# The retention's output product of a two-layer decoder as one block product of seven, behind the second gates

## The chip, the core and the metric

The kernel runs on one core of a Trainium2 chip. What is measured is the device time in microseconds (us) of one execution. A core has a matrix engine (TensorE, PE in the profile), a vector engine (VectorE, DVE), a scalar engine (ScalarE, ACT), a general engine (GpSimd, POOL) and a queue engine that starts transfers (SyncE, SP). Each engine works off its own instructions in a fixed order and waits on semaphores for the others.

## The reference

Two layers over 512 tokens with a width of 1024, all in fp32. Each layer mixes an attention branch and a retention branch through two gates, and a feed-forward part of width 4096 follows. The change touches the product of the retention's result `r` with `w_b`, and what stands around it:

```python
h = rmsnorm(x, g_mix)
z = h @ w_in
aq, ak, av, rq, rk, rv, rg, ga, gb = jnp.split(z, SPLIT_POINTS, axis=-1)
...
r = chunkwise_retention(rq, rk, rv)
r = r * lax.rsqrt(jnp.mean(r * r, axis=-1, keepdims=True) + EPS)
r = r.reshape(B, S, RET_V) * jax.nn.silu(rg.astype(jnp.float32))
yb = r.astype(x.dtype) @ w_b

mixed = jax.nn.sigmoid(ga) * ya + jax.nn.sigmoid(gb) * yb
x = x + mixed @ w_out
```

## The kernel before

Activations lie transposed: features on the 128 partitions, in 8 chunks of 128 features, and the 512 tokens along a row. A fp32 product is made of three matrix products of rounded parts: each operand is split into `hi` (rounded) and `lo` (the rest), and hi·hi, hi·lo and lo·hi are added up (`products`, lines 391 to 393).

**Weights.** They arrive in units of 128x1024 (512 KB), in the order of the list `order`. SP starts the load of a unit into a `raw` tile (five of them), four units ahead of the one that is split; ACT writes `hi` (line 339), DVE writes `lo` (line 340), each with four buffers, so that splitting stays up to three units ahead of PE. Units that are sums of others are made in two ways: DVE adds two raw tiles (line 319), or POOL sums blocks in DRAM in the course of the run, from a list of jobs (`sum_steps`), and SP loads the result.

**Products of seven.** Three products of the kernel already multiply 2x2 blocks with seven block products in place of eight: the values `rv` (function `values`), the feed-forward's first product (name `pair`) and its second (name `block`). They need forms of the moving operand, that is, sums and differences of its four blocks (two halves of the features by two halves of the tokens). For `values` the class `Turned` builds them: `load` fetches the input, `build` makes the sums on DVE (lines 892 to 895) and splits them, on ACT (line 411) and DVE (line 412).

**Retention.** Heads go in two pairs. Each of a pair's two heads ends in `norm` and `finish`: the squares `sq`, their split `sh` and `sl`, a column sum on PE (`ssq`, line 569), a square root on ACT (`inv`, line 570), a reciprocal on DVE (line 571), two products each (lines 1067 and 1068) and the split of the result (`r<-z` or `late<-z`, lines 411 and 412). This work runs as a generator in the background: every `chunk` of a foreground product advances it by some steps (its last argument is the rate), and `drain()` runs it to its end.

**The piece that is changed**, in each layer: the last two chunks of `rg`, with the second pair of heads as background; gates 0 to 3 (`chunk("w_in", ...)` with `gate`, which evacuates PSUM on DVE at line 827 and takes the sigmoid on ACT at line 828); `w_b` for output chunks 0 to 3 as a group over the eight input chunks, in the middle of which `second_pair` drains the retention; gates 4 to 7; `w_b` for chunks 4 to 7 one after the other; then `x` (which at this time holds the gated attention branch, `mixed`) is loaded again from DRAM, and `w_out` follows. Each `w_b` matmul has a 128x128 weight block and all 512 tokens moving, and there are 8 x 8 x 3 = 192 of them per layer. `put_mixed` multiplies the result by the gate (line 1176), adds the attention branch (1177) and splits the sum (411, 412).

The order of each engine's instructions is not written out: a scheduler of the framework sets it from its own estimates and from the order of the code, with `tc.issue_after` as a bound in a few places. On the chip each engine keeps to the order so found.

## Time and profile before

| what | us |
|---|---|
| median of 3 runs (1467.56 to 1468.66) | 1468.51 |
| the profiled execution | 1466.77 |
| its span, first to last instruction | 1465.0 |
| DVE busy | 1124.7 |
| ACT busy | 944.6 |
| POOL busy | 209.0 |

The span is what the profile sees of an execution; 1.8 us of the profiled one lie around it. A row of a group reads: line, engine, operation, output<-inputs, shapes, count, then the busy time, the mean duration of one in ns, and the engine's idle time before them with what ended it. A row of the timeline reads: start in us, duration in us, engine, line, operation, and in brackets the idle time of the engine before it and what ended that. Matmuls overlap, so their durations are longer than the distance from one start to the next.

### The profile page before, as it was taken

Reading aid. Unit: us, or ns where it says so; the run is one execution under the profiler, and the core shown is the slowest. Engines: PE = TensorE matmul, PEld = TensorE weight load, DVE = VectorE, ACT = ScalarE, POOL = GpSimd, SP = SyncE. Lnnn points to the kernel's source line nnn. Section 1 sums busy time; section 2 is a strip of 40 time slices with the busy share of each in tenths; the row PEclk is TensorE's granted clock in tenths of the full one; section 3 lists DMA queues with packets and bytes.
Section 4 is the critical chain, followed back from the end, with each engine's and each line's share of the span. In section 5 each row is a group of like instructions: output and inputs, shape, how many; then the busy total and the mean of one; then the engine's idle time right before and its main releaser. Section 6 shows DMA issues by size and latency. Waiting matters only on the chain.

```text
span 1465.0 us, 21388 instructions
## 1 busy us (share of the span) xinstructions
PE 1453.4 (99%) x7751; PEld 1256.2 (86%) x7751; DVE 1124.7 (77%) x1697; ACT 944.6 (64%) x1549; POOL 209.0 (14%) x302
## 2 busy tenths in 40 slices
...
GB/s 263 182 295 207 114 152 259 200 207 290 228 57 193 195 188 199 181 172 188 297 172 191 291 212 104 181 251 189 228 272 101 99 197 199 196 189 199 180 186 140
DMA packets 95867, 287.32 MB, mean 196 GB/s; under 512 B 11152, under 2 KB 11280, under 8 KB 90896
## 3 DMA queue, kind: packets, MB, share of 16 engines
...
q8 instruction: 61, 1.00, 0.3%
...
## 4 chain that ended last, share of the span: by engine, by line
PE 97%; DMA 1%; ACT 1%; DVE 0%; issue 0%; SPq 0%; DVEq 0%; ACTq 0%
PE mm L391 25%; PE mm L393 25%; PE mm L392 25%; PE b L391 3%; PE b L392 3%; PE b L393 3%; PE rv L391 2%; PE rv L392 2%; PE rv L393 2%; PE mm L406 1%; PE score L774 1%; PE pT L739 1%; PE r L393 1%; PE r L392 1%; PE r L391 1%; DMA y<-eu 1%
## 5 line engine op out<-in xcount | busy, mean ns | idle before, releaser
L339 ACT ACTIVATE hi<-raw 128x1024 fp32r<-128x1024 f32 (+1 forms) x375 | 382.3, 1020 | 285.3 <-PE mm L392 166.0
L340 DVE TENSOR_TENSOR lo<-raw,hi 128x1024 fp32r<-128x1024 f32 (+1 forms) x376 | 439.2, 1174 | 144.6 <-ACT hi L339 143.2
L391 PE MATMUL mm<-xh,hi 128*128 128x512 f32 (+1 forms) x976 | 344.1, 355 | 1.0 <-ACT xh L414 1.0
L392 PE MATMUL mm<-xl,hi 128*128 128x512 f32 (+1 forms) x976 | 344.0, 355 | 0.0
L393 PE MATMUL mm<-xh,lo 128*128 128x512 f32 (+1 forms) x976 | 341.9, 355 | 0.0
L393 PE MATMUL mm<-r,lo 128*128 128x256 f32 (+1 forms) x736 | 239.2, 325 | 0.5 <-DVE lo L340 0.5
L392 PE MATMUL mm<-r,hi 128*128 128x256 f32 (+1 forms) x736 | 239.3, 325 | 0.0
L391 PE MATMUL mm<-r,hi 128*128 128x256 f32 (+1 forms) x736 | 236.6, 325 | 0.5 <-ACT mm L1343 0.5
L391 PEld LDWEIGHTS mm<-xh,hi 128*128 128x128 f32 x976 | 184.8, 189 | 25.6 <-ACT xh L414 1.4
L392 PEld LDWEIGHTS mm<-xl,hi 128*128 128x128 f32 x976 | 184.9, 189 | 24.2
L393 PEld LDWEIGHTS mm<-xh,lo 128*128 128x128 f32 x976 | 183.9, 189 | 23.6
L391 PEld LDWEIGHTS mm<-r,hi 128*128 128x128 f32 x736 | 139.9, 190 | 13.7 <-ACT mm L1343 0.7
L392 PEld LDWEIGHTS mm<-r,hi 128*128 128x128 f32 x736 | 139.9, 190 | 13.2
L393 PEld LDWEIGHTS mm<-r,lo 128*128 128x128 f32 x736 | 139.9, 190 | 12.1 <-DVE lo L340 0.7
L1488 POOL DMA_DIRECT2D y<-eu x56 | 62.4, 1358 | 369.1 <-DVE eu L1473 369.1
L392 PE MATMUL mm<-lo,r 128*128 128x512 f32 (+1 forms) x276 | 104.4, 388 | 0.0
L393 PE MATMUL mm<-hi,r 128*128 128x512 f32 (+1 forms) x276 | 101.2, 387 | 0.0
L391 PE MATMUL mm<-hi,r 128*128 128x512 f32 (+1 forms) x276 | 98.7, 391 | 0.5 <-ACT r L411 0.2
L391 PE MATMUL b<-hi,r 128*128 128x512 f32 x180 | 70.5, 392 | 0.0
L392 PE MATMUL b<-lo,r 128*128 128x512 f32 x180 | 70.3, 391 | 0.0
L393 PE MATMUL b<-hi,r 128*128 128x512 f32 x180 | 67.9, 390 | 0.0
L1488 POOL DMA_DIRECT2D y<-y x56 | 55.6, 1007 | 78.7 <-ACT y L1483 73.5
...
## 6 DMA issues: line engine op xcount, KB each, us to landing
...
```

The lines of the kernel that those rows point to most:

```text
L339: state["high"] = nc.scalar.activation(hi[:, at], raw[:, at], AF.Copy).ins
L340: nc.vector.tensor_tensor(lo[:, at], raw[:, at], f32(hi[:, at]), ALU.subtract)
L391: nc.tensor.matmul(ps, ah, bh, start=start and i == 0, stop=False, **more)
L392: nc.tensor.matmul(ps, ah, bl, start=False, stop=False, **more)
L393: latest[0] = nc.tensor.matmul(ps, al, bh, start=False, stop=stop and i == n - 1, **more).ins
L406: latest[0] = nc.tensor.matmul(ps, w[:, cols(j, c)], moving[k][low], start=first, stop=bool(final)).ins
L739: nc.tensor.transpose(pt[:, i * P : (i + 1) * P], sm[:, at : at + P], ident)
L774: nc.tensor.matmul(ps[:, g * w : (g + 1) * w], q_s[g][:, c, at], part[:, keys], start=i == 0, stop=i == 1)
L1488: nc.gpsimd.dma_start(y[:, 2 * j + m, i * T : (i + 1) * T], t, **how)
```

## The change

The product with `w_b` becomes one product of seven block products, with 256 tokens moving in each matmul. The weight units of `w_b` come in the list `order` behind all of `w_in` under the name `wb`, 14 per layer: part 0 to 6, two units each. Parts 2 and 4 are made by DVE from raw tiles, parts 1 and 5 come from sums that POOL makes in DRAM (two more jobs per layer), parts 0, 3 and 6 are loaded as they are. Gates 0 to 3 and the last two chunks of `rg` advance the background by 1.5 steps per chunk, and the retention is drained behind gate 3; gates 4 to 7 follow in front of the product. Between them `again(0)` and `again(2)` build the forms of the retention's results: two DVE additions put hi and lo of the first pair's results together again, the second pair's results are there in fp32 in the tile that held `rg`, and `Turned.build` makes and splits the sums. `mixing` runs the seven products into three PSUM accumulators `a`, `b` and `c` of two banks each, and writes the mixed result in four quarters (`put`), from the forms and from plain quarters of `r` (`outputs`).

```diff
     order = [("w_in", i) for i in range(4 + 2 + 8 + 2 + 4 + 2 + 2)]
     order += [("w_a", i) for i in range(4)]
     order += [("rv", part, u) for part in range(7) for u in range(2)]
-    order += [("w_in", i) for i in range(24, 34)]
-    order += [("w_b", i) for i in range(4)]
-    order += [("w_in", i) for i in range(34, 38)]
-    order += [("w_b", i) for i in range(4, 8)]
+    order += [("w_in", i) for i in range(24, 38)]
+    order += [("wb", part, u) for part in range(7) for u in range(2)]
     order += [("w_out", i) for i in range(8)]
...
-    sums_rv = [dram.tile([2, P, 2 * UNIT], F32, name=f"sums_rv{l}") for l in range(DEPTH)]
+    MIXING = {"rv": w_rv, "wb": w_wb}
+    sums_mix = {
+        name: [dram.tile([2, P, 2 * UNIT], F32, name=f"sums_{name}{l}") for l in range(DEPTH)] for name in MIXING
+    }
...
+        for name, at in (("rv", 0), ("wb", 5)):
+            jobs[at:at] = [(sums_mix[name][layer][u], MIXING[name][layer, u], 2 * UNIT) for u in range(2)]
...
+        at = {0: 0, 1: 1, 3: 3, 5: 0, 6: 2}[part]
+        source = sums_mix[name][layer][u] if part in (1, 5) else MIXING[name][layer, u]
...
-            def build(self, ks):
-                for part, b in enumerate(self.b):
+            def build(self, ks, scaled=True):
+                two_b = self.b.pop(ks)
+                for part, b in enumerate(two_b if scaled else ()):
                     for i in range(2):
                         col = g_mix * KD + ks + 4 * part + i
                         nc.scalar.activation(b[:, i, :], b[:, i, :], AF.Copy, scale=gain[:, col : col + 1])
-                (b11, b12), (b21, b22) = ((b[:, :, :H], b[:, :, H:]) for b in self.b)
+                (b11, b12), (b21, b22) = ((b[:, :, :H], b[:, :, H:]) for b in two_b)
...
-                split(hi, lo, self.b[1].rearrange("p a (b t) -> p b a t", t=H))
...
-        rg, rg_next = {}, {}
         def put_rg(i):
             def put(ps):
                 if i % 2 == 0:
                     two = big("z")
                     rg[i], rg_next[i + 1] = two[:, 0, :], two[:, 1, :]
+                    rg_both[i] = two
...
         drain()
         background.append(retention(1))
         for i in (6, 7):
-            chunk("w_in", layer, xs, put_rg(i))
+            chunk("w_in", layer, xs, put_rg(i), 1.5)
         gates = []
 
-        def gate_tile(c):
-            if c % 2 == 0:
-                two = big("gb")
-                gates.extend(two[:, j, :] for j in range(2))
-
-        for c in range(4):
-            gate_tile(c)
-            chunk("w_in", layer, xs, gate(gates[c]))
-
-
+        def put_gates(cs, rate=1.0):
+            for c in cs:
+                if c % 2 == 0:
+                    gates.append(big("gb"))
+                chunk("w_in", layer, xs, gate(gates[c // 2][:, c % 2, :]), rate)
+
+        put_gates(range(4), 1.5)
+        drain()
+
+
+        turned = Turned()
+        turned.take()
+
+        def again(ks):
+            first = big("xg")
+            for i in range(2):
+                hi, lo = (f32(view(s)) for s in ret[ks + i])
+                nc.vector.tensor_tensor(first[:, i, :], hi, lo, ALU.add)
+            turned.b[ks] = [first, rg_both.pop(4 + ks)]
+            turned.build(ks, False)
+
+        put_gates((4,))
+        again(0)
+        put_gates((5, 6))
+        again(2)
+        put_gates((7,))
         ms = {}
 
-        def put_mixed(c):
-            def put(ps):
-                m = temp("m")
-                nc.vector.tensor_tensor(m, ps, gates[c], ALU.mult)
-                nc.vector.tensor_tensor(m, m, mixed[c], ALU.add)
-                pace(m)
-                hi, lo = slots.one(), slots.one()
-                split(view(hi), view(lo), m)
-                ms[c] = (hi, lo)
-
-            return put
-
-        rT = []
-
-        def second_pair():
-            drain()
-            rT.extend(tuple(view(s) for s in ret[k]) for k in range(4, KD))
-
-        rT.extend(tuple(view(s) for s in ret[k]) for k in range(4))
-        group("w_b", layer, rT, [put_mixed(c) for c in range(4)], {1: second_pair})
-        for c in range(4, KD):
-            gate_tile(c)
-            chunk("w_in", layer, xs, gate(gates[c]))
-        for c in range(4, KD):
-            chunk("w_b", layer, rT, put_mixed(c))
-        for k in range(KD):
-            slots.give(*ret.pop(k))
-
-
-        for c in range(KD):
-            nc.sync.dma_start(x[:, c, :], source[:, c, :])
+        def mixing(turned):
+
+            a, c = ([bank(ps_mm, "wb") for _ in range(2)] for _ in range(2))
+            b = [bank(pool, "wb") for pool in (ps_mm, ps_aux)]
+            nc.tensor.matmul(b[1], ones, xh[:, 0, :], start=True, stop=True)
+
+            def outputs(half, tokens):
+                at = slice(tokens * H, tokens * H + H)
+                return [tuple(view(s)[:, at] for s in ret[k]) for k in range(4 * half, 4 * half + 4)]
+
+            def multiply(ps, moving, start=True):
+                for u in range(2):
+                    hi, lo = unit("wb", layer)
+                    for k in range(2):
+                        vh, vl = moving[2 * u + k]
+                        for n in range(4):
+                            o = ps[n // 2][:, (n % 2) * H : (n % 2 + 1) * H]
+                            cols = slice(k * T + n * P, k * T + (n + 1) * P)
+                            first, final = u == 0 and k == 0, u == 1 and k == 1 and n % 2 == 1
+                            for w, v in ((hi, vh), (hi, vl), (lo, vh)):
+                                latest[0] = nc.tensor.matmul(
+                                    o,
+                                    w[:, cols],
+                                    v,
+                                    start=start and first and n % 2 == 0 and w is hi and v is vh,
+                                    stop=final and w is lo,
+                                    skip_group_check=True,
+                                ).ins
+
+            def both(t):
+                return t.rearrange("p (a t) -> p a t", t=H)
+
+            def keep(ps, sign):
+                got = []
+                for m in range(2):
+                    t = temp("kept")
+                    nc.scalar.activation(t, ps[m], AF.Copy, scale=float(sign))
+                    got.append(both(t))
+                return got
+
+            def put(i, j, ps, sign, kept=None):
+                at = slice(j * H, j * H + H)
+                for m in range(2):
+                    n = 2 * i + m
+                    if n not in ms:
+                        ms[n] = slots.four()
+                    t = ms[n][0]
+                    v, g, p = both(temp("m")), gates[n][:, :, at], both(ps[m])
+                    if kept:
+                        nc.vector.scalar_tensor_tensor(kept[m], p, float(sign), kept[m], ALU.mult, ALU.add)
+                        nc.vector.tensor_tensor(v, kept[m], g, ALU.mult)
+                    elif sign < 0:
+                        nc.vector.scalar_tensor_tensor(v, p, -1.0, g, ALU.mult, ALU.mult)
+                    else:
+                        nc.vector.tensor_tensor(v, p, g, ALU.mult)
+                    nc.vector.tensor_tensor(v, v, x[:, 2 * n : 2 * n + 2, at], ALU.add)
+                    pace(v[:, 0, :])
+                    split(t[:, 0:2, at], t[:, 2:4, at], v)
+
+            def load(i):
+                for c in range(4 * i, 4 * i + 4):
+                    nc.sync.dma_start(x[:, c, :], source[:, c, :])
+
+            multiply(a, outputs(0, 0))
+            for m in range(2):
+                nc.scalar.activation(b[m], a[m], AF.Copy)
+            multiply(c, turned[1])
+            five = keep(c, -1)
+            multiply(b, turned[2], False)
+            turned.free(0)
+            two = keep(b, 1)
+            multiply(a, outputs(1, 0), False)
+            put(0, 0, a, 1)
+            multiply(c, outputs(1, 1), False)
+            for k in range(KD):
+                slots.give(*ret.pop(k))
+            put(0, 1, c, 1, two)
+            load(0)
+            multiply(b, turned[3], False)
+            put(1, 1, b, -1, five)
+            multiply(b, turned[4], False)
+            turned.free(1)
+            put(1, 0, b, -1)
+            load(1)
+
+        mixing(turned)
 
...
-        mT = [tuple(view(s) for s in ms[k]) for k in range(KD)]
+        mT = [tuple(ms[k // 2][0][:, n + k % 2, :] for n in (0, 2)) for k in range(KD)]
...
-def _value_blocks(w):
+def _mixing_blocks(w):
+        "w_rv": _stack(w_in, lambda w: _mixing_blocks(w[:, O_RV : O_RV + D])),
-        "w_b": _stack(w_b, _half_grouped),
+        "w_wb": _stack(w_b, _mixing_blocks),
```

Where instructions move, on three engines, in the first layer (the second has the same rows but for a few neighbours). Names end in the number of their buffer; line numbers are those of the kernel that the rows are of (the splits at 339, 340 and 412 before are 336, 337 and 409 in the changed one).

On DVE, from the second reciprocal of the second pair of heads on. Before, its results (`z_2496`) are multiplied and split, with weight units in between (`lo`), and the first `w_b` chunks are gated:

```order
L571 RECIPROCAL inv_2814<-inv_2814 128x512
L1067 TENSOR_TENSOR z_2496<-z_2496,inv_2814 128x512 x2
L1068 TENSOR_TENSOR z_2496<-rr_2668,z_2496 128x512 x2
L340 TENSOR_TENSOR lo_2923<-raw_2808,hi_2922 128x1024
L412 TENSOR_TENSOR r4_85<-z_2496,r4_85 128x512
L827 TENSOR_TENSOR gb_2978<-mm_2985,rstd_313 128x512
L412 TENSOR_TENSOR r4_85<-z_2496,r4_85 128x512
L340 TENSOR_TENSOR lo_2982<-raw_2844,hi_2981 128x1024
L1176 TENSOR_TENSOR m_2950<-mm_2804,gb_2572 128x512
```

The rows of the change from the same reciprocal to the first split form and the last gates (`xg_2862` is the first pair's part of the forms, `t2_2865` the first form that a product reads, `r5_86` the tile of its split):

```order
L568 RECIPROCAL inv_2743<-inv_2743 128x512
L337 TENSOR_TENSOR lo_2960<-raw_2829,hi_2959 128x1024
L1066 TENSOR_TENSOR z_2514<-z_2514,inv_2743 128x512 x2
L316 TENSOR_TENSOR raw_2829<-raw_2829,raw_2736 128x1024
L1067 TENSOR_TENSOR z_2514<-rr_2637,z_2514 128x512 x2
L337 TENSOR_TENSOR lo_3004<-raw_2876,hi_3003 128x1024
L1177 TENSOR_TENSOR xg_2862<-late_89 128x512
L1177 TENSOR_TENSOR xg_2862<-r7_88 128x512
L409 TENSOR_TENSOR r4_85<-z_2514,r4_85 128x512 x2
L316 TENSOR_TENSOR raw_2876<-raw_2876,raw_2783 128x1024
L337 TENSOR_TENSOR lo_3035<-raw_2829,hi_3034 128x1024
L890 TENSOR_TENSOR z_1601<-z_1601,xg_2862 128x2x256
```

```order
L337 TENSOR_TENSOR lo_3066<-raw_2876,hi_3065 128x1024
L891 SCALAR_TENSOR_TENSOR t2_2865<-xg_2862,z_1601 128x512
L892 TENSOR_TENSOR xg_2862<-xg_2862 128x2x256
L893 SCALAR_TENSOR_TENSOR z_1601<-t2_2865,z_1601 128x2x256
L409 TENSOR_TENSOR r5_86<-t2_2865,r5_86 128x512
L409 TENSOR_TENSOR r5_86<-xg_2862,r5_86 128x512
L409 TENSOR_TENSOR r3_84<-z_1601,r3_84 128x1024
L824 TENSOR_TENSOR gb_2913<-mm_2918,rstd_315 128x512
L824 TENSOR_TENSOR gb_2913<-mm_2963,rstd_315 128x512
```

Between the reciprocal and the split of the first form stand four weight units, two additions of raw tiles, the second head's results and the additions of the forms; the gates 6 and 7 (`mm_2918`, `mm_2963`) are evacuated behind that split.

On PE, where the first product of seven ends. The product `a` (`wb_2994`, `wb_2995`) reads plain quarters of the first pair's results; what follows at once is `b` (`wb_2998`, `wb_2999`) with the first split form, and then `c` (`wb_2996`):

```order
L389 MATMUL mm_2963<-xl_77,hi_2831 128x512
L390 MATMUL mm_2963<-xh_76,lo_2832 128x512
L1192 MATMUL wb_2999<-xh_76,ones_117 128x512
L1208 MATMUL wb_2994<-late_89,hi_2878 128x256 x2
L1208 MATMUL wb_2994<-late_89,lo_2879 128x256
```

```order
L1208 MATMUL wb_2995<-r1_82,hi_2914 128x256 x2
L1208 MATMUL wb_2995<-r1_82,lo_2915 128x256
L1208 MATMUL wb_2998<-r5_86,hi_3034 128x256
L1208 MATMUL wb_2999<-r5_86,hi_3034 128x256
L1208 MATMUL wb_2998<-r5_86,hi_3034 128x256
L1208 MATMUL wb_2998<-r5_86,lo_3035 128x256
```

Before, `w_b` starts there with rows such as these (the last two rows of gate 3, and the first of the group over chunks 0 to 3), in front of gates 4 to 7:

```order
L392 MATMUL mm_2773<-xl_77,hi_2575 128x512
L393 MATMUL mm_2773<-xh_76,lo_2576 128x512
L391 MATMUL mm_2804<-late_89,hi_2650 128x512
L392 MATMUL mm_2804<-late_89,hi_2650 128x512
L393 MATMUL mm_2804<-late_89,lo_2651 128x512
```

So the seven products stand behind gate 7 (`mm_2963`), and the second of them reads a form.

On ACT, from the split of the first head's results to the square root of the second head. Before:

```order
L411 ACTIVATE late_89<-z_1599 128x512
L339 ACTIVATE hi_2892<-raw_2767 128x1024
L570 ACTIVATE inv_2814<-ssq_2815,x_75 128x512
L339 ACTIVATE hi_2922<-raw_2808 128x1024
L411 ACTIVATE r4_85<-z_2496 128x512 x2
```

and now:

```order
L408 ACTIVATE late_89<-z_1601 128x512
L336 ACTIVATE hi_2914<-raw_2783 128x1024
L825 ACT_TABLE_LOAD
L825 ACTIVATE gb_2828<-gb_2828 128x512 x2
L567 ACT_TABLE_LOAD
L567 ACTIVATE inv_2743<-ssq_2744,x_75 128x512
L336 ACTIVATE hi_2959<-raw_2829 128x1024
```

The sigmoids of gates 4 and 5 stand between the two square roots, with a load of a function table on each side.

37 lines of the change are left out of this document (15 added, 22 removed).

## The prediction

> **What bounds the kernel now.** I read the page first: the engines' busy time, then the chain that ended last.
>
> ```profile
> span 1465.0 us, 21388 instructions
> PE 1453.4 (99%) x7751; PEld 1256.2 (86%) x7751; DVE 1124.7 (77%) x1697; ACT 944.6 (64%) x1549; POOL 209.0 (14%) x302
> ...
> PE 97%; DMA 1%; ACT 1%; DVE 0%; issue 0%; SPq 0%; DVEq 0%; ACTq 0%
> ```
>
> PE sets the time: it is busy for 99% of the span and makes 97% of the chain. Matmuls taken away are won, and a wait of PE is lost in full. What a matmul costs is its distance to the next start, not its duration. From the timeline of PE, the first and the last row of seven matmuls with 512 tokens moving and of ten with 256:
>
> ```profile
> 899.43 0.39 PE L393 MATMUL mm<-r,lo 128*128 128x512 f32 x1
> ...
> 900.79 0.39 PE L393 MATMUL mm<-r,lo 128*128 128x512 f32 x1
> ```
> ```profile
> 579.75 0.28 PE L393 MATMUL mm<-r,lo 128*128 128x256 f32 x1
> ...
> 580.83 0.28 PE L393 MATMUL mm<-r,lo 128*128 128x256 f32 x1
> ```
>
> Six distances in 1.36 us are 0.227 us each, nine in 1.08 us are 0.120 each. Half the tokens thus cost 53%, so seven products in place of eight save less than an eighth.
>
> DVE is second, and its load by stage matters more than its mean. The stretches of the first layer around the change:
>
> ```profile
> core 0: us, PE busy (x) PEld busy (x) DVE busy (x) ACT busy (x) POOL busy (x), PEclk, DMA share, GB/s
> 259.00:300.00 41.00, 41.00 (x202) 34.94 (x201) 29.95 (x45) 22.65 (x36) 7.04 (x12) 1.00 0.74 207
> 300.00:320.00 20.00, 20.00 (x89) 16.42 (x89) 17.06 (x17) 8.57 (x12) 3.00 (x6) 1.00 0.97 249
> 320.00:340.00 20.00, 20.00 (x90) 16.49 (x89) 15.16 (x22) 9.68 (x12) 4.30 (x8) 1.00 0.61 190
> 340.00:366.00 26.00, 26.00 (x115) 21.28 (x114) 13.00 (x17) 8.04 (x10) 5.55 (x9) 1.00 1.02 300
> ```
>
> From 300 to 320, while the retention ends, DVE is busy for 17.06 of 20 us. Just there the change adds work.
>
> **What PE saves.** Removed per layer are 192 matmuls of 512: 192 x 0.227 = 43.5 us. Added are 7 products x 2 units x 24 = 336 of 256, and one to open a PSUM bank: 336 x 0.120 + 0.2 = 40.5. The difference is 3.0 us per layer, 6.0 in both.
>
> **What DVE and ACT get.** Durations by group and form:
>
> ```profile
> L340 DVE TENSOR_TENSOR lo<-raw,hi 128x1024 fp32r<-128x1024 f32 x342 | 416.9, 1222 | 128.1 <-ACT hi L339 126.7 <-DMA r<-qlo 0.2
> L571 DVE RECIPROCAL inv<-inv 128x512 f32<-128x512 f32 x8 | 26.8, 3351 | 12.4 <-ACT inv L570 12.4
> L1067 DVE TENSOR_TENSOR z<-z,inv 128x512 f32<-128x512 f32 x16 | 10.3, 685 | 0.0
> L319 DVE TENSOR_TENSOR raw<-raw 128x1024 f32<-128x1024 f32 x8 | 9.8, 1225 | 0.2
> L412 DVE TENSOR_TENSOR r<-xg,r 128x1024 fp32r<-128x1024 f32 x4 | 4.9, 1222 | 0.0
> L954 DVE SCALAR_TENSOR_TENSOR kept<-rv,rcol,kept 128x512 f32<-128x512 f32 x4 | 2.8, 743 | 0.0
> ```
>
> Per layer DVE gets six more unit splits (14 units for 8; 6 x 1.22 = 7.3 us), four additions of raw tiles (4 x 1.225 = 4.9), the forms in two builds, each with two additions, four sums and two splits at 0.69 and one split at 1.22 (2 x 6.7 = 13.5), and four operations on kept results (3.0): 28.7 us. The gates, products and splits behind them only move. ACT gets the `hi` halves, copies and table loads, some 15 us; it is at half load. In sum DVE has room: the rows show 4.8 us idle from 320 to 340 and 13.0 from 340 to 366. What counts is the order in which it comes.
>
> **Where PE will wait.** The rows of the second pair's end in the first layer, from the timelines of PE, ACT and DVE:
>
> ```profile
> 295.37 0.39 PE L391 MATMUL mm<-late,hi 128*128 128x512 f32 x1
> ...
> 312.15 0.39 PE L569 MATMUL ssq<-sl,ones 128*128 128x512 f32 x1
> ```
> ```profile
> 308.12 0.63 ACT L411 ACTIVATE late<-z 128x512 fp32r<-128x512 f32 x1 [1.05 <-DVE z L1068]
> 308.72 1.06 ACT L339 ACTIVATE hi<-raw 128x1024 fp32r<-128x1024 f32 x1
> 312.57 0.69 ACT L570 ACTIVATE inv<-ssq,x 128x512 f32<-128x512 f32 x1 [2.79 <-PE ssq L569]
> ...
> 321.28 1.28 ACT L828 ACT_TABLE_LOAD   x1
> 322.58 0.64 ACT L828 ACTIVATE gb<-gb 128x512 f32<-128x512 f32 x1
> ```
> ```profile
> 300.65 3.35 DVE L571 RECIPROCAL inv<-inv 128x512 f32<-128x512 f32 x1 [2.99 <-ACT inv L570]
> 303.92 0.63 DVE L1056 TENSOR_TENSOR sq<-sq 128x512 f32<-128x512 f32 x1
> ...
> 313.30 3.35 DVE L571 RECIPROCAL inv<-inv 128x512 f32<-128x512 f32 x1 [2.25 <-ACT inv L570]
> ...
> 319.10 1.22 DVE L340 TENSOR_TENSOR lo<-raw,hi 128x1024 fp32r<-128x1024 f32 x1
> 320.24 0.69 DVE L412 TENSOR_TENSOR r<-z,r 128x512 fp32r<-128x512 f32 x1
> 320.84 0.69 DVE L827 TENSOR_TENSOR gb<-mm,rstd 128x512 f32<-128x512 f32 x1
> ```
>
> Back to back, DVE's instructions start 0.09 us closer than they last: 3.27 for a reciprocal, 1.14 for 128x1024, 0.60 for 128x512.
>
> *When PE arrives.* Where `w_b` began (295.37) gate 4 now begins. Up to the first new product PE does four gates (96 x 0.227 = 21.8 us), the last 12 matmuls of the retention (as long as 7.5 of 512 tokens: 1.7), four column sums (0.9) and the opening one (0.2): 24.6 us, so the products start at 320.0. The first, `a`, reads plain results, takes 48 x 0.120 = 5.8 us and ends at 325.8. Next on PE is `b`, which needs the first split form.
>
> *When that form is ready.* The column sum keeps its place (312.4). ACT now has the sigmoids of gates 4 and 5 between the two square roots, each time with a table load: `hi` ends at 309.8, then 1.28 for a load, two sigmoids (1.2), 1.28 for a load, and hand-overs with DVE of some 0.4: the root runs from 314.0 to 314.7 instead of 312.57, and the reciprocal starts at 314.75 instead of 313.30. From there to the split of the form, the order of DVE shows the reciprocal (3.27), four unit splits and two raw additions (6 x 1.14 = 6.8), and 13 instructions of 512 elements (four products, two splits of results, two additions, four sums, and the split asked for: 7.8): 17.9 us without a gap. It is done at 332.65, and PE waits 332.65 - 325.8 = 6.8 us.
>
> The second layer goes the same way:
>
> ```profile
> 1021.34 0.40 PE L391 MATMUL mm<-late,hi 128*128 128x512 f32 x1
> ```
> ```profile
> 1036.19 1.22 DVE L340 TENSOR_TENSOR lo<-raw,hi 128x1024 fp32r<-128x1024 f32 x1
> 1037.33 0.69 DVE L412 TENSOR_TENSOR r<-z,r 128x512 fp32r<-128x512 f32 x1
> ...
> 1039.71 3.35 DVE L571 RECIPROCAL inv<-inv 128x512 f32<-128x512 f32 x1 [1.09 <-ACT inv L570]
> ```
>
> The products start at 1021.34 + 24.6 = 1045.95 and `a` ends at 1051.7. DVE evacuates gates 4 and 5 behind the unit split of 1036.19, from 1037.3 to 1038.5; ACT's first table load waits for the first of them at 1037.9, and load, sigmoids, load and root end near 1042.4. The reciprocal moves from 1039.71 to 1042.5, and with the same 17.9 us the form is there at 1060.4: a wait of 8.7 us.
>
> *What is late next.* `c` needs two PSUM banks that gates 6 and 7 hold, and DVE evacuates these 2.9 us behind the form's split (two splits, then the gates); the 24 matmuls of `b`'s first half take as long, so nothing is added. The unit split that comes next on DVE is due some 0.5 us too late in each layer. Afterwards units come at 2.9 us of PE each while DVE needs 1.14 per unit and about 1 for forms: it catches up, and `w_out` finds its operand.
>
> **The clock of PE.** The eight warming matmuls at the start of the run, beside four at full speed, and the longest pause later:
>
> ```profile
> 1.06 3.53 PE L371 MATMUL warm<-ones 128*128 128x512 f32 x8 [1.06 <-DVE ones L366]
> ```
> ```profile
> 320.18 1.07 PE L391 MATMUL mm<-r,hi 128*128 128x512 f32 x4
> ```
> ```profile
> 738.83 0.44 PE L1554 MATMUL turn<-ident,y 128*128 128x128 f32 x2 [1.16 <-DMA y<-eu]
> ```
>
> Eight cost 3.53 us where full speed makes it 1.07 + 4 x 0.227 = 1.98: an idle PE begins slowly and loses 1.55 us. A pause of 1.16 us later has no row of a lower clock behind it. A wait of 7 to 9 us lies between these; it is far longer than any pause of the run, so I take the full 1.5 us for each of the two waits, with 0 as the lower bound.
> [...]
>
> [...]
>
> **The sum** against the profiled execution (1466.77): -6.0 for the matmuls, +6.8 and +8.7 for the waits on the form, +1.0 for the splits, +3.0 for the clock: +13.5, so 1480.3. The median shown lies 1.7 us above that execution, hence **1482**. Bounds: the waits are at least 0, if the forms came in time; upwards, each hand-over between ACT and DVE (five or so in a layer) may cost as much as the 0.4 us of the root's, 2 us per layer; the clock costs 0 to 3.0.
>
> **Rivals.**
> - *Same wait, full clock*: 1479. For it speaks the pause of 1.16 us; against it, its length.
> - *The forms come in time*, the faster side: only the 6.0 us count, 1462.5. It holds if the split of the first form ends by 325.8, that is, if 6.8 us of the 17.9 (8.7 in the second layer) ran before the reciprocal, in the 2.25 us of idle time that DVE has there. Only the first head's results enter this form, so the data allow it. Against it stands DVE's fixed order, in which the reciprocal comes first.
> - *A shorter wait*: it eats the saving and little more, 1468 (1465 to 1474). It would need the gates and loads on ACT not to delay the root (1.4 us and 2.8) and shorter hand-overs than I think; the rows of DVE leave little room.
> - *The weights come too late*: the new units are read every 2.9 us, where `w_b`'s took 24 x 0.227 = 5.4. From 340 to 366 the transfers are at a share of 1.02 already. Units loaded four ahead have 11.6 us to arrive. Against it: 4 of the 14 are not loaded at all, and `values` has such units with 12 matmuls of 512 each, one every 2.7 us, in a run whose PE is never idle for long. If four or five units were 2 us late in each layer: 1490 to 1500.
>
> **How the numbers follow.** Forecast 0.50 (its own range 1479 to 1488), full clock 0.17, in time 0.09, shorter wait 0.11, weights 0.13. The range 1467 to 1491 leaves out the case in time, a part of the shorter wait and most of the weights, about 2 in 10. This kernel's times tell 0.2% (3 us) from no change: below 1465.6 lie the case in time and 0.02 of the shorter wait, 0.11; 0.05 lies within; 0.84 above.
>
> **What would show it.** In the changed profile PE should stop for about 7 and 9 us behind the first 48 matmuls of the product, released by DVE's split of the first form; the second reciprocal should start some 1.5 and 2.8 us later than before; DVE should be without a gap from it to that split. Matmuls at double distance behind the stop would show the clock. No stop, or one released by a transfer, would prove the forecast wrong; so would a product that takes much more than 40.5 us of matmuls.

## The result, and the profile after

| | before | after |
|---|---|---|
| median of 4 runs, us | 1468.03 (1466.12 to 1468.66) | 1484.12 (1482.64 to 1485.17) |
| ratio, 95% interval | | 1.0111 [1.0096, 1.0126] |
| span of the profiled execution, us | 1465.0 | 1481.8 |

The change costs 16 us. The page after, with the engines' busy time and the chain that ended last:

```profile
span 1481.8 us, 22114 instructions
PE 1453.2 (98%) x8041; PEld 1268.6 (86%) x8041; DVE 1174.9 (79%) x1761; ACT 978.3 (66%) x1589; POOL 214.0 (14%) x314
...
PE 94%; DVE 3%; DMA 1%; ACT 1%; issue 1%; SPq 0%; DVEq 0%; ACTq 0%
```

PE's modelled busy time has hardly moved and the span is 16.8 us longer: the loss is waiting and slow running, not matmuls. DVE, which had no share of the chain, now has 3% of it, some 40 us: the way back from PE's stops leads through DVE's queue. From the timeline of PE, the stops of the first layer and then of the second:

```profile
325.75 0.28 PE L1208 MATMUL wb<-r,lo 128*128 128x256 f32 x1
332.13 0.79 PE L1208 MATMUL wb<-r,hi 128*128 128x256 f32 x2 [6.10 <-ACT r L408]
333.40 0.58 PE L1208 MATMUL wb<-r,hi 128*128 128x256 f32 x1 [0.47 <-DVE r L409]
333.78 0.41 PE L1208 MATMUL wb<-r,lo 128*128 128x256 f32 x1
333.99 0.63 PE L1208 MATMUL wb<-r,hi 128*128 128x256 f32 x2
...
364.09 0.28 PE L1208 MATMUL wb<-r,lo 128*128 128x256 f32 x1
365.92 1.20 PE L388 MATMUL mm<-r,hi 128*128 128x512 f32 x4 [1.55 <-ACT r L408]
...
1059.93 0.28 PE L1208 MATMUL wb<-r,lo 128*128 128x256 f32 x1
1068.07 0.79 PE L1208 MATMUL wb<-r,hi 128*128 128x256 f32 x2 [7.86 <-ACT r L408]
...
1100.48 0.47 PE L1208 MATMUL wb<-r,hi 128*128 128x256 f32 x2 [0.90 <-DVE kept L1237]
```

The last matmul of `a` starts at 325.75 and the first of `b` at 332.13: 6.38 us where 0.12 is regular, a stop of 6.26. It is released by ACT's `hi` of the first form; two matmuls later PE stops again until DVE has written the `lo`. The row at 333.78 is followed at 0.21 us, not 0.12, at a granted clock of 0.50. A later stop, which nobody had foreseen, stands in both layers ahead of the last 48 of the product's 336 matmuls; it is called the stop near the end below. In the first layer four matmuls of `w_out`, which the scheduler placed there, wait 1.55 us until ACT has split their operand. In the second the seventh block product itself waits 0.90 us until DVE has read its bank. DVE's and ACT's rows of the first layer:

```profile
315.30 3.35 DVE L568 RECIPROCAL inv<-inv 128x512 f32<-128x512 f32 x1 [2.59 <-ACT inv L567]
318.57 1.16 DVE L337 TENSOR_TENSOR lo<-raw,hi 128x1024 fp32r<-128x1024 f32 x1
...
332.06 0.69 DVE L893 SCALAR_TENSOR_TENSOR z<-t,z 128x512 f32<-128x512 f32 x1
332.66 0.68 DVE L409 TENSOR_TENSOR r<-t,r 128x512 fp32r<-128x512 f32 x1
```
```profile
310.81 1.28 ACT L825 ACT_TABLE_LOAD   x1
312.11 1.16 ACT L825 ACTIVATE gb<-gb 128x512 f32<-128x512 f32 x2
313.28 1.28 ACT L567 ACT_TABLE_LOAD   x1
314.57 0.69 ACT L567 ACTIVATE inv<-ssq,x 128x512 f32<-128x512 f32 x1
...
365.25 1.25 ACT L408 ACTIVATE r<-m 128x512 fp32r<-128x512 f32 x2
```

The reciprocal waits for the root, the root for two sigmoids between two table loads; no instruction of DVE between 318.57 and 332.66 has an idle time before it. The clock is seen best in windows of 3.41 us:

```profile
core 0: us, PE busy (x) PEld busy (x) DVE busy (x) ACT busy (x) POOL busy (x), PEclk, DMA share, GB/s
325.03:328.45 3.42, 1.00 (x9) 0.80 (x7) 3.42 (x5) 1.58 (x3) 0.00 (x0) 1.00 0.94 201
328.45:331.86 3.41, 0.00 (x0) 0.00 (x0) 3.38 (x5) 1.05 (x2) 0.00 (x0) 0.50 0.81 251
331.86:335.27 3.41, 2.66 (x10) 2.37 (x11) 3.41 (x6) 1.89 (x3) 0.00 (x0) 0.50 0.14 56
335.27:338.69 3.42, 3.42 (x18) 3.42 (x18) 3.35 (x6) 2.84 (x4) 0.33 (x1) 0.50 0.01 2
338.69:342.10 3.41, 3.41 (x30) 3.41 (x30) 2.98 (x5) 1.87 (x3) 1.62 (x3) 1.00 0.57 135
362.58:365.99 3.41, 1.86 (x16) 1.66 (x15) 3.41 (x6) 1.70 (x3) 0.03 (x1) 1.00 1.01 157
```

The granted clock is 0.50 for exactly three such windows, 328.45 to 338.69, and 6.6 us of them lie behind the stop. The stop at 364 brings no low clock.

**How the runs are compared.** The start of a run varies by some 2 us (the stretch below begins at 224.50 in after, at 226.82 in e_plain), so each layer is measured by itself, from its last `rv` matmul to its first `b` matmul. Of before and of after:

```profile
224.52 0.39 PE L393 MATMUL rv<-hi,r 128*128 128x512 f32 x1
437.29 0.40 PE L391 MATMUL b<-hi,r 128*128 128x512 f32 x1
```
```profile
224.50 0.39 PE L390 MATMUL rv<-hi,r 128*128 128x512 f32 x1
445.49 0.39 PE L388 MATMUL b<-hi,r 128*128 128x512 f32 x1
```

212.77 us became 220.99: +8.2. The same two rows of the second layer (950.47 and 1164.80, now 958.65 and 1181.58) give +8.6. Together that is the span's 16.8. Within this stretch two things are added up from PE's timeline: *stops*, distances between starts of 256-token matmuls longer than the regular 0.120 by over 0.2 us (in the first layer of e_pooladd and in both layers of e_warm also one of 1.7 us behind a 512-token matmul), and *slow*, what distances of 0.20 to 0.225 have over 0.120. After: stops 9.3 and 10.4, slow 2.2 and 1.4.

### The profile page after: what moved, and what is told of

Read it like the earlier page. It is cut to its first block, busy times and chain, and to the rows that moved or that the text cites. A ratio compares the mean times of both kernels' runs of the same rounds, so it can differ in the third digit from the quotient of the medians.

```text
span 1481.8 us, 22114 instructions
## 1 busy us (share of the span) xinstructions
PE 1453.2 (98%) x8041; PEld 1268.6 (86%) x8041; DVE 1174.9 (79%) x1761; ACT 978.3 (66%) x1589; POOL 214.0 (14%) x314
## 3 DMA queue, kind: packets, MB, share of 16 engines
q8 instruction: 63, 1.03, 0.3%
## 4 chain that ended last, share of the span: by engine, by line
PE 94%; DVE 3%; DMA 1%; ACT 1%; issue 1%; SPq 0%; DVEq 0%; ACTq 0%
PE mm L388 23%; PE mm L390 23%; PE mm L389 23%; PE wb L1208 4%; PE b L388 3%; PE b L389 3%; PE b L390 3%; PE rv L388 2%; PE rv L389 2%; PE rv L390 2%; PE mm L403 1%; DVE lo L337 1%; PE score L771 1%; PE pT L736 1%; PE r L389 1%
## 5 line engine op out<-in xcount | busy, mean ns | idle before, releaser
L337 DVE TENSOR_TENSOR lo<-raw,hi 128x1024 fp32r<-128x1024 f32 (+1 forms) x388 | 454.0, 1176 | 144.9 <-ACT hi L336 143.7
L336 ACT ACTIVATE hi<-raw 128x1024 fp32r<-128x1024 f32 (+1 forms) x387 | 395.1, 1022 | 258.9 <-PE mm L389 121.3
L389 PE MATMUL mm<-xl,hi 128*128 128x512 f32 (+1 forms) x976 | 343.7, 355 | 0.0
L388 PE MATMUL mm<-r,hi 128*128 128x256 f32 (+1 forms) x608 | 187.9, 311 | 2.0 <-ACT r L408 1.6
L390 PE MATMUL mm<-r,lo 128*128 128x256 f32 (+1 forms) x608 | 189.1, 311 | 0.6 <-DVE lo L337 0.6
L389 PE MATMUL mm<-r,hi 128*128 128x256 f32 (+1 forms) x608 | 189.0, 311 | 0.0
L388 PEld LDWEIGHTS mm<-r,hi 128*128 128x128 f32 x608 | 115.6, 190 | 10.3 <-ACT r L408 1.8
L389 PEld LDWEIGHTS mm<-r,hi 128*128 128x128 f32 x608 | 115.7, 190 | 7.9
L390 PEld LDWEIGHTS mm<-r,lo 128*128 128x128 f32 x608 | 115.8, 190 | 7.1 <-DVE lo L337 0.8
L1208 PE MATMUL wb<-r,hi 128*128 128x256 f32 x400 | 76.9, 294 | 15.8 <-ACT r L408 14.0
L1208 PEld LDWEIGHTS wb<-r,hi 128*128 128x128 f32 x400 | 65.4, 201 | 17.1 <-ACT r L408 14.4
L388 PE MATMUL b<-hi,r 128*128 128x512 f32 x180 | 70.4, 391 | 0.0
## 6 DMA issues: line engine op xcount, KB each, us to landing
sums_down<-w_down_in POOLq DMA_DIRECT2D x30, 1024.0 KB, 11.1
```

Of the source, the lines that this page charges most:

```text
L336: state["high"] = nc.scalar.activation(hi[:, at], raw[:, at], AF.Copy).ins
L337: nc.vector.tensor_tensor(lo[:, at], raw[:, at], f32(hi[:, at]), ALU.subtract)
L388: nc.tensor.matmul(ps, ah, bh, start=start and i == 0, stop=False, **more)
L389: nc.tensor.matmul(ps, ah, bl, start=False, stop=False, **more)
L390: latest[0] = nc.tensor.matmul(ps, al, bh, start=False, stop=stop and i == n - 1, **more).ins
L1208: latest[0] = nc.tensor.matmul(o, w[:, cols], v, start=start and first and n % 2 == 0 and w is hi and v is vh, stop=final and w is lo, ski ...
```

## The experiments

All are the changed kernel with one edit unless something else is said; the time before was 1466.1 to 1467.8 in the runs beside them. The change of a layer is against before.

| run | median us | ratio [95%] | layer 1 / 2 | stops | slow |
|---|---|---|---|---|---|
| after | 1484.12 | 1.0111 [1.0096, 1.0126] | +8.2 / +8.6 | 9.3 / 10.4 | 2.2 / 1.4 |
| e_noforms | 1460.74 | 0.9966 [0.9955, 0.9977] | -3.4 / -3.4 | 0 / 0 | 0 / 0 |
| e_plain | 1483.24 | 1.0106 [1.0091, 1.0121] | +6.2 / +7.9 | 6.4 / 8.2 | 2.8 / 2.7 |
| e_root | 1480.29 | 1.0090 [1.0075, 1.0105] | +5.6 / +6.4 | 7.3 / 7.6 | 1.4 / 2.0 |
| e_noadd | 1479.89 | 1.0094 [1.0077, 1.0111] | +5.1 / +8.0 | 6.6 / 8.7 | 1.7 / 2.4 |
| e_norecip | 1477.59 | 1.0072 [1.0055, 1.0088] | +4.8 / +3.8 | 5.2 / 4.6 | 2.7 / 2.0 |
| e_half | 1484.57 | 1.0121 [1.0106, 1.0136] | +7.1 / +8.5 | 8.2 / 10.0 | 2.0 / 1.5 |
| e_pooladd | 1483.76 | 1.0119 [1.0104, 1.0134] | +8.0 / +7.5 | 9.8 / 9.3 | 1.2 / 1.3 |
| e_warm | 1481.00 | 1.0096 [1.0075, 1.0118] | +4.4 / +8.8 | 2.7 / 4.0 | 0.2 / 1.5 |
| e_formsfirst | 1486.19 | 1.0130 [1.0115, 1.0146] | +8.3 / +10.3 | 9.5 / 10.9 | 2.0 / 2.4 |
| e_order | 1490.51 | 1.0161 [1.0145, 1.0176] | +9.7 / +13.4 | 11.1 / 12.6 | 1.7 / 3.8 |
| b3 | 1490.84 | 1.0156 [1.0139, 1.0173] | +10.0 / +12.6 | 10.8 / 12.9 | 2.2 / 2.7 |
| b1 | 1479.92 | 1.0095 [1.0073, 1.0117] | +4.6 / +5.2 | 4.3 / 6.0 | 1.7 / 2.3 |

In nearly every row the layer's change is -3.4, plus stops, plus slow, to 0.6 us (after: -3.4 + 9.3 + 2.2 = 8.1 for 8.2). The -3.4 is e_noforms, in which PE never stops. Two rows have a further part, told below: e_warm its filler, b1 a late operand of the retention.

### Without the forms: what PE alone saves

**e_noforms**

```diff
-        again(0)
...
-        again(2)
...
-            multiply(c, turned[1])
+            multiply(c, outputs(0, 1))
-            multiply(b, turned[2], False)
+            multiply(b, outputs(0, 0), False)
...
-            multiply(b, turned[3], False)
+            multiply(b, quarter(1, 1), False)
-            multiply(b, turned[4], False)
+            multiply(b, quarter(1, 0), False)
```

> No forms of the retention's results are built, and the four products that read forms read plain quarters (of the retention's results and of the normed input: wrong sums come out; weights, matmuls, gates and the four quarters of the result are as in the change). DVE-budget theory (from the second head's reciprocal to the last quarter, some 55 us, DVE is busy without a pause, so PE's time there is DVE's work): DVE loses 13.5 us of work per layer, and PE's stops vanish but for the unit splits: 1463 to 1467. Transfer theory (weights arrive too late): 1478 or more.

Its page has the same matmuls as after, and DVE's work less the forms:

```profile
span 1458.7 us, 22070 instructions
PE 1447.6 (99%) x8041; PEld 1264.7 (87%) x8041; DVE 1150.8 (79%) x1725; ACT 967.5 (66%) x1577; POOL 216.0 (15%) x314
```

Both stops, the half clock and the stop near the end are gone, though the fourteen units, their splits and the additions of raw tiles are all still there. So the weights are not the cause, and the product by itself saves 6.8 us in the two layers, a little more than its 6.0. The forms are 24 us of DVE's work (1174.9 less 1150.8), and the span is 23 us longer with them (1481.8 less 1458.7).

**e_plain** keeps this work and lets only the first two products read plain quarters, so that nothing waits for the first forms.

```diff
-            multiply(c, turned[1])
+            multiply(c, outputs(0, 1))
-            multiply(b, turned[2], False)
+            multiply(b, outputs(0, 0), False)
```

> The second and third of the seven products read plain quarters of the retention's results in place of split forms (wrong sums come out; the forms are still built, and the other two products that need forms still read them). DVE-queue theory (the form is late because everything on DVE between the second reciprocal and the form is in one queue, unit splits and raw additions too): PE still stops behind the first 48 matmuls, but only until the unit split of the next product, some 3.3 us in the first layer and 4 to 5 in the second, so too short for much of a slower clock; total 1471 to 1478. If the form alone is late: no stop, 1462 to 1465. If the weights arrive too late: the stop stays, above 1480.

It did not come to that: 1 us of the median was won, 2.0 and 0.7 us of the two layers. From PE's timeline, the stops of its first layer:

```profile
331.44 0.58 PE L1208 MATMUL wb<-late,lo 128*128 128x256 f32 x1 [1.91 <-DVE lo L337]
...
364.80 0.47 PE L1208 MATMUL wb<-r,hi 128*128 128x256 f32 x2 [3.20 <-DVE kept L1237]
```

The first is released by a weight unit's split, which stands in the same queue of DVE, the second by the sums at the product's end, which come later in it. A form that nobody waits for still delays what stands behind it. So the form's date alone is not the cause; the queue is.

### The length of the queue ahead of the first form

**e_root** lets the second root run ahead of the two sigmoids: from gate 4 on a sigmoid may not be issued before the last root.

```diff
+    last_root = [None]
...
-        nc.scalar.activation(dest, ps, AF.Sqrt, bias=eps, scale=1.0 / n)
+        last_root[0] = nc.scalar.activation(dest, ps, AF.Sqrt, bias=eps, scale=1.0 / n).ins
...
-                nc.scalar.activation(dest, dest, AF.Sigmoid)
+                with tc.issue_after(last_root[0]) if late_gates else ExitStack():
+                    nc.scalar.activation(dest, dest, AF.Sigmoid)
...
+        late_gates.append(1)
...
         put_gates((4,))
```

> The sigmoids of gates 4 to 7 are put behind the second head's square root on ACT, so that no function table is loaded between the two roots. DVE's order is unchanged. Theory: the second reciprocal starts about 2.0 us earlier in the first layer and 2.5 in the second, the stop of PE is shorter by the same, the slow stretch behind it stays: 1479.5 (1478 to 1481). Rival (the date of the reciprocal does not matter, because DVE's other work fills the time anyway): 1484 within 1.

As expected. From the timelines of DVE and of PE:

```profile
314.80 3.35 DVE L570 RECIPROCAL inv<-inv 128x512 f32<-128x512 f32 x1 [0.43 <-ACT inv L569]
```
```profile
331.86 0.80 PE L1213 MATMUL wb<-r,hi 128*128 128x256 f32 x2 [4.16 <-ACT r L408]
...
1064.44 0.80 PE L1213 MATMUL wb<-r,hi 128*128 128x256 f32 x2 [5.07 <-ACT r L408]
```

The stage begins 1.67 us later in this run (226.17 for 224.50), so the reciprocal is 2.2 us earlier in it. The first stops are 4.32 and 5.22 us long where they were 6.26 and 8.02: shorter by 1.9 and 2.8, about what the root was moved. The root's delay was a part of the wait, and two thirds of the wait are not the root.

**e_noadd** loads parts 2 and 4 in place of adding raw tiles on DVE; two of the four additions stand ahead of the first form.

```diff
-        if part in (2, 4):
+        if part in (2, 4) and name == "rv":
...
-        at = {0: 0, 1: 1, 3: 3, 5: 0, 6: 2}[part]
-        source = sums_mix[name][layer][u] if part in (1, 5) else MIXING[name][layer, u]
+        at = {0: 0, 1: 1, 2: 0, 3: 3, 4: 0, 5: 0, 6: 2}[part]
+        source = sums_mix[name][layer][u] if part in (1, 2, 4, 5) else MIXING[name][layer, u]
```

> The weight units that DVE makes by adding two raw tiles (parts 2 and 4) are loaded from DRAM instead, from another part's sums (wrong sums come out). DVE loses 4 x 1.22 = 4.9 us per layer, and 2 MB more are moved per layer. DVE-budget theory: two of the additions stand in front of the first form, so the first stop is 2.3 us shorter, and the rest is won behind it: 3 to 5 us per layer, a total 6 to 10 us under the change (about 1482 in these runs), 1472 to 1476. If the transfers are the limit, more of them make it slower than the change.

It missed its time by 4 us. The rows of PE:

```profile
329.02 0.79 PE L1208 MATMUL wb<-r,hi 128*128 128x256 f32 x2 [2.81 <-ACT r L408]
331.43 0.58 PE L1208 MATMUL wb<-r,hi 128*128 128x256 f32 x1 [1.61 <-DVE r L409]
```

The first stop is 3.3 us shorter (2.97), more than the two additions last, because a unit's split also came to stand between the sum and its `lo`; but for that `lo` PE waits again, 1.91 us where it was 0.77, since only the first matmuls can do with the `hi` half. DVE's row of that split starts at 330.69, 2 us earlier than after's: about what the two additions last, and no more. In the second layer only 0.6 us in all was won: the first stop is shorter there too (4.61 for 8.02), but the wait for the `lo`, the stop near the end and the slow part are longer.

**e_norecip** leaves out the reciprocal of the second head of the second pair (3.27 us of DVE).

```diff
-        nc.vector.reciprocal(dest, dest)
+        if whole:
+            nc.vector.reciprocal(dest, dest)
...
-                inverse_rms(self.parts, RET_V, self.inv)
+                inverse_rms(self.parts, RET_V, self.inv, self.h != 3)
```

> The reciprocal of the last head of the second pair is left out (its results are scaled wrongly; all else is computed). DVE loses one instruction of 3.3 us per layer, in front of both pairs of forms, and its order behind it changes by one unit split. Theory as it stands after the runs before (what counts is DVE's work from the second head's root to the forms; what stands behind them has room): the first form is ready 3.9 us earlier, PE stops for about 2.5 us in the first layer and 4.5 in the second instead of 6.3 and 8.0, and the clock stays up at least in the first: 1471 to 1476. If the second pair of forms or the weight units are as late as the first form by themselves, PE stops there instead: 1479 or more.

The first stop fell to 1.87 and 1.90 us, and it is no longer the form that ends it, but ACT's copy of `a`:

```profile
328.36 0.38 PE L1209 MATMUL wb<-r,hi 128*128 128x256 f32 x1 [1.71 <-ACT wb L1254]
```

With the reciprocal out of its way, and two unit splits and an addition of raw tiles that the scheduler moved behind it, DVE's sum for the first form starts at 324.73, 6 us earlier than after's, so PE meets the next date instead: the copy, then the `lo`, then the second forms (1.52 us at 343.7). The time is a little above the range that was expected; stops this short still lowered the clock (below).

### Work behind the first form

**e_half** leaves out the second build of the forms, which lies behind the first.

```diff
-        again(2)
...
+            for n in range(1, 5):
+                for k in range(2):
+                    turned.parts[n, 2 + k] = turned.parts[n, k]
```

> Only the first pair of forms is built; the products read it in place of the second pair too (wrong sums come out). What stands in front of the first stop is as in the change; behind it DVE loses 6.8 us of work per layer. First-stop theory (the loss is the wait on the first form and the slow clock behind it): only the stops near the end go, 1477 to 1481. DVE-budget theory (DVE's work between the second reciprocal and the last quarter sets when the product ends, wherever PE waits): about 6 us less per layer, 1467 to 1471.

No gain. On DVE a gap appears behind the form, and PE's stop is longer than in after, not shorter:

```profile
345.35 1.23 DVE L337 TENSOR_TENSOR lo<-raw,hi 128x1024 fp32r<-128x1024 f32 x1 [6.67 <-ACT hi L336]
```
```profile
335.79 1.78 PE L1207 MATMUL wb<-r,hi 128*128 128x256 f32 x5 [7.36 <-ACT r L408]
```

The time is above both ranges. The stop is 7.51 us, 1.25 more than after, because the scheduler put the evacuations of two gates (0.6 us each) ahead of the form. DVE's total load is refuted as the cause: with one of the two builds gone DVE is idle for 6.67 us in one piece, and the loss is where it was. Only the stop near the end is gone.

**e_pooladd** gives the last addition of each mixed result to POOL.

```diff
-                    nc.vector.tensor_tensor(v, v, x[:, 2 * n : 2 * n + 2, at], ALU.add)
+                    nc.gpsimd.tensor_tensor(v, v, x[:, 2 * n : 2 * n + 2, at], ALU.add)
```

> The eight additions of the attention branch to the gated product per layer go from DVE to POOL (8 x 0.60 = 4.8 us of DVE's time). They all stand behind the stop. DVE-budget theory: the first stop stays as it is, but the stop of 1.7 and 1.1 us near the end goes away and w_out's first splits come earlier: 2 to 5 us in all, 1477 to 1480. First-stop theory (only what stands in front of the form counts): 1482 within 1.

The first stop did not move (6.25 and 8.03), as the theory of the first stop had it, but the time, 1483.76, lies above both ranges. Of the gain expected behind the stop only the second layer has a part: its stop near the end is gone. In the first, `w_out`'s operands are late. From the groups of the whole run:

```profile
L1243 POOL TENSOR_TENSOR m<-m,x 128x512 f32<-128x512 f32 x16 | 28.9, 1825 | 36.3 <-DVE m L1242 23.7 <-DVE m L1238 9.0 <-DVE m L1240 2.2
```

And one group of the stretch from 350 to 376, in this run and then in after:

```profile
L409 DVE TENSOR_TENSOR r<-m,r 128x512 fp32r<-128x512 f32 x5 | 5.6, 1115 | 0.2 <-ACT r L408 0.2
```
```profile
L409 DVE TENSOR_TENSOR r<-m,r 128x512 fp32r<-128x512 f32 x5 | 3.4, 692 | 0.0
```

POOL takes 1.83 us in the mean for what DVE does in 0.69, and DVE's splits of the same results take 1.12 us in the mean and not 0.69: those that overlap one of POOL's additions take some 1.77 (DVE's row of 355.14, beside POOL's of 351.93 to 356.36), the others 0.69. What DVE was spared it paid back in longer operations: its busy time in the whole run is 1178.9 us, with 16 instructions fewer, and 1174.9 in after.

### Another order

**e_order** puts the two products that need no form, `a` and its second half, first: 96 matmuls, 11.5 us, cover the first form. The units come in that order, and parts 1 and 2 alternate.

```diff
-    order += [("wb", part, u) for part in range(7) for u in range(2)]
+    order += [("wb", *u) for u in ((0, 0), (0, 1), (3, 0), (3, 1), (1, 0), (2, 0), (1, 1), (2, 1))]
+    order += [("wb", part, u) for part in (4, 5, 6) for u in range(2)]
...
-            def multiply(ps, moving, start=True):
-                for u in range(2):
+            def multiply(ps, moving, start=True, us=(0, 1)):
+                for u in us:
...
-            multiply(c, turned[1])
+            multiply(a, outputs(1, 0), False)
+            for u in range(2):
+                multiply(c, turned[1], True, (u,))
+                multiply(b, turned[2], False, (u,))
...
-            multiply(b, turned[2], False)
...
-            multiply(a, outputs(1, 0), False)
```

> The order of the seven products is changed: the second product into a, which reads plain quarters, comes directly behind the first, so that PE has 96 instead of 48 matmuls that need no form (5.8 us more); the weight units follow in that order, and DVE's work stays the same. First-stop theory: the first stop shrinks from 6.3 and 8.0 us to 1 to 3 (the copy of a by ACT included), the clock stays up, and nothing else moves: 1467 to 1471. DVE-budget theory: the stops move behind it, to the second pair of forms and the unit splits, and only the 2 us in which DVE itself was idle come back: 1477 to 1483.

Both expectations were wrong. The large first stop is gone, and others, 11.1 us in sum, stand elsewhere, most of it where the second pair's forms are read. The first of these:

```profile
343.79 0.51 PE L1217 MATMUL wb<-r,hi 128*128 128x256 f32 x2 [3.31 <-ACT r L417]
```

DVE's split of that second form starts at 347.04 (341.72 in after), at the end of a stretch from 326 on in which DVE is never idle. The units wanted earlier stand ahead of the second forms now. The edit also moves the loads: one unit of sums from DRAM is loaded only when an addition of DVE has freed a raw tile (SP's row of 329.76), and ACT waits for it, 1.83 us in the first layer (row 334.14) and 3.29 in the second (1073.31), where DVE then waits 1.19 for ACT. In after ACT waits for no transfer around the product.

**b3** is e_order with the edit of e_root.

> The order of products of the run before it, and no table load between the two square roots: right results. First-stop theory: no stop is left, 1462 to 1466, under the kernel before. DVE-budget theory: DVE starts its stretch without a pause 2.0 to 2.8 us earlier, and the product ends as much earlier: 1473 to 1479.

It missed as well, with 1490.84. Here the late unit costs more. From ACT's timeline:

```profile
335.70 1.06 ACT L345 ACTIVATE hi<-raw 128x1024 fp32r<-128x1024 f32 x1 [3.51 <-DMA raw<-sums_wb]
```

DVE then waits 1.42 us for this `hi`, and PE stops 1.89 us for a gate whose evacuation stands behind that unit in DVE's queue. In the second layer ACT waits 6.14 us for the unit, DVE 4.04, and that stop of PE is 5.21 us (in e_order 1.07 and 0.83). So e_order and b3 do not try the order of the products by itself: a part of their loss is a late transfer.

**e_formsfirst** turns the other piece: the first head's forms are built before the second head's norm, which waits for them (with the edit of e_root).

```diff
+            if pair == 1:
+                two[0].finish()
+                yield
+                turned_r.append(Turned())
+                turned_r[0].take()
+                again(0)
+                yield
+            with tc.issue_after(last_form[0]) if pair else ExitStack():
+                two[1].norm()
...
-            for head in two:
+            for head in two[pair:]:
...
-        again(0)
```

> The first pair of forms is built in front of the second head's reciprocal (the first head is finished first, and the reciprocal is queued behind the last split of that form). Queue-order theory in its narrow sense (the forms only stand in the wrong place): PE does not stop any more, 1462 to 1466. DVE-load theory (from the first reciprocal to the last form DVE has more work than PE gives it time for, wherever the forms stand): the wait is cut into shorter ones, on the evacuation of gate 4, on unit splits and on the second pair of forms, 5 to 8 us per layer in sum, each too short for the clock to fall: 1470 to 1477.

The DVE-load theory had the places, but not the sum (5 to 8 us) nor the clock, which fell in both layers. The first form is in time, and PE stops for gates, units, second forms and near the end instead, ten stops of 0.2 to 2.1 us in the first layer, 9.5 in sum. The first of them:

```profile
325.17 0.50 PE L1223 MATMUL wb<-late,hi 128*128 128x256 f32 x2 [1.60 <-DVE gb L826]
```

Four kernels with the same forms built (after, e_order and e_formsfirst, which order the work differently, and e_plain, in which PE does not wait for the first forms) have stops of 9.3, 11.1, 9.5 and 6.4 us in the first layer, at different places.

### The clock

**e_warm** lets PE multiply into a bank nobody reads yet (20 and 28 matmuls of 512 tokens) while it would wait for the first form.

```diff
             multiply(a, outputs(0, 0))
+            for _ in range((20, 28)[layer]):
+                nc.tensor.matmul(b[1], ones, xh[:, 0, :], start=True, stop=True)
```

> Twenty (first layer) and 28 (second) matmuls of 512 with no use are put behind the first product into a bank that is overwritten, to fill most of the stop of PE. Clock theory: the matmuls behind the stop run at 0.120 us from start to start instead of 0.213, which saves 2.4 to 2.9 us per layer: 1479 (1478 to 1481). Rival (the distance of 0.213 comes from operands that arrive late, from DVE or ACT): 1484 within 1, and 0.213 stays.

Half of it came true. In the first layer the clock holds and the slow part falls from 2.2 to 0.2 us. In the second the clock falls:

```profile
330.00:336.00 6.00, 3.97 (x17) 2.75 (x16) 5.97 (x9) 3.33 (x5) 0.00 (x0) 1.00 0.69 212
...
1064.00:1070.00 6.00, 3.69 (x17) 2.95 (x16) 5.93 (x10) 3.44 (x5) 0.00 (x0) 0.82 0.38 122
```

(The columns are those of the windows above.) In both layers the filler ends ahead of the form's date, 2.8 and 2.7 us before it is complete. In the first this gap is spread over two windows of 3.41 us, which PE fills to 63% and 55% by the count below; in the second it lies in one, filled to 20%. The fillers, at 0.227 us each, take 4.5 and 6.4 us of the wait and shorten nothing. Of the 3.9 us that the first layer wins back, 2.0 are the clock and 1.7 the stop near the end, which is gone because the scheduler placed 24 matmuls of `w_out` ahead of the last 48 of the product, and not four.

The expectations of e_plain, e_order, e_norecip, e_formsfirst and b1 take stops of up to 5 us to be too short for the clock. No run had shown that, and in all five it fell in both layers (slow 1.7 to 3.8 us).

Why stops of under 2 us lower the clock in e_norecip, while the one of 1.71 near the end of after does not (its window, 362.58 to 365.99, is filled to 50%), e_norecip's windows of 3.41 us show:

```profile
325.35:328.77 3.42, 1.68 (x12) 1.28 (x11) 3.42 (x5) 2.22 (x4) 0.00 (x0) 1.00 0.99 202
328.77:332.18 3.41, 2.63 (x12) 2.63 (x13) 3.41 (x6) 2.21 (x4) 0.00 (x0) 0.50 0.89 293
...
1055.81:1059.22 3.41, 1.69 (x15) 1.48 (x13) 3.41 (x5) 2.18 (x3) 0.00 (x0) 1.00 1.00 204
1059.22:1062.63 3.41, 1.23 (x6) 0.84 (x7) 3.41 (x5) 3.21 (x4) 0.00 (x0) 1.00 0.94 239
1062.63:1066.04 3.41, 3.41 (x19) 3.41 (x18) 3.41 (x5) 0.38 (x1) 0.00 (x0) 0.50 0.57 192
```

In after the clock changes at 328.45, 338.69, 1062.31 and 1072.55 us: on one grid of such windows, 0, 3, 215 and 218 times 3.4133 us behind the first. In e_norecip it falls at 328.77 and 1062.63, 215 windows apart too. In these runs the falls follow the matmuls that a window holds, not the length of one stop. Their count times 0.120 us (0.227 for those of 512 tokens), cut at the window's edges, fills 37% of the window from 325.35, and the next is at half clock; 44% from 1055.81, and the clock stays; 18% from 1059.22, and it falls. Of the windows that begin between 320 and 345 us, one in each of eleven runs (none in e_noforms and e_warm) had the clock fall behind it. It was filled to at most 43% (b1, from 328.97), and all others at full clock to 45% (b3, from 335.43) or more.

### A version that should have gained

**b1** has the edit of e_root, and parts 2 and 4 summed in DRAM by POOL's transfers, so that DVE adds no raw tiles.

```diff
+    sums_wb2 = [[dram.tile([P, 2, UNIT], F32, name=f"sums_wb2_{l}_{u}") for u in range(2)] for l in range(DEPTH)]
...
+                    nc.gpsimd.dma_start(to, two[0].unsqueeze(1).broadcast_to([P, 2, UNIT]))
+                    yield
+                    nc.gpsimd.dma_start(to, two[1].unsqueeze(1).broadcast_to([P, 2, UNIT]), accum_op=ALU.add)
+                    nc.gpsimd.dma_start(to[:, 1, :], w[:, 3 * UNIT : 4 * UNIT], accum_op=ALU.add)
...
+        if part in (2, 4):
+            nc.sync.dma_start(raw, sums_wb2[layer][u][:, part // 2 - 1, :])
+            return
```

> Two of the reliefs together, with right results: no table load between the two square roots, and parts 2 and 4 summed by POOL in DRAM ahead of time, so that DVE adds no raw tiles (5 MB more are moved per layer). DVE-budget theory: the first stop is 6.3 - 2.0 - 2.3 = 2 us in the first layer and 8.0 - 2.8 - 2.3 = 3 in the second, short enough that the clock stays up, and 2.3 us of DVE's time are won behind it: 1466 to 1471, about the kernel before. If the added transfers collide with the weights: above 1474.

The stops are halved (4.3 and 6.0; the profiled run is the fastest of the four), the time is 1479.92, above the range, and its runs spread from 1476.3 to 1484.8. A new wait of PE stands in the retention; its row and DVE's:

```profile
271.86 0.33 PE L401 MATMUL ret<-r 128*128 128x128 f32 x1 [1.45 <-DVE s L1044]
```
```profile
271.11 1.16 DVE L1044 TENSOR_TENSOR s<-ret,dm 128x512 f32<-128x512 f32 x2 [6.16 <-DMA dm<-decay_in]
```

DVE waits for the load of `dm`, which is issued at 258.0 as in after and lands 13.1 us later, in after 4.8. From 258 to 272 the transfers' share is 1.03 here and 0.33 in after, so the added transfers are the likely cause; no run takes them out alone. Of all the runs only e_noforms, which leaves the forms out, is faster than before; with all of the work done, b1 and e_root come nearest.

## Why the prediction was right, point by point

The forecast was 1482 in 1467 to 1491, and slower; it came to 1484.1. The mechanism is the one predicted. By its terms, against the profiled execution:

| term | predicted | measured |
|---|---|---|
| matmuls saved | -6.0 | -6.8 (e_noforms) |
| first stop, layer 1 | +6.8 | +6.26 |
| first stop, layer 2 | +8.7 | +8.02 |
| behind the first stop ("splits") | +1.0 | +2.6 |
| the clock | +3.0 | +3.6 |
| stop near the product's end | 0 | +2.8 |
| sum | +13.5 | +16.4 (span +16.8) |

That the sum comes so near is in part luck: the matmuls and the first stops came out 2.0 us lower than forecast, the other terms 4.9 us higher.

- *When PE arrives.* Predicted 325.8 and 1051.7 in before's time; the last matmul of `a` ends its 0.12 us at 325.87. In the second layer, where everything is 8.2 us later, it is 1060.05, and 1051.9 without these.
- *When the form is ready.* Predicted 332.65, on time with the reciprocal at 314.75. The reciprocal starts at 315.30, 0.55 later, as the root does: ACT's `hi` ahead of the first table load ended at 310.8, not 309.8, and only half of that was made good by shorter hand-overs. The split ends at 333.34. The prediction erred in what PE waits for: the first matmuls need only the `hi`, which ACT writes before DVE has done the `lo`. So the first stop ends at 332.13, earlier than forecast, and the rest of the form's date appears as a second stop behind it.
- *The root.* ACT's rows have it at 314.57 to 315.26 for 314.0 to 314.7 predicted, between two table loads of 1.28 us. e_root confirms its part of the wait. The load delays the sigmoid by its 1.28 and 0.02 more: 310.81 + 1.28 is 312.09, and the sigmoid starts at 312.11.
- *"A late unit split, 0.5 a layer"* was the wrong name: the 1.29 us behind each first stop are the wait for the `lo` (0.77) and two distances of 0.38 us at the low clock. No unit's split releases PE there.
- *The clock.* 23 and 15 matmuls at 0.21 us, 1.8 times the regular 0.12 and not double, cost 2.15 and 1.40 us, against twice 1.5. That the full value applies was right; e_warm shows that it is the clock. The 1.5 was the loss of eight matmuls of 512 at the start of the run, so the nearness of the size is luck.
- *"It catches up, and `w_out` finds its operand"* is the step that failed. PE has done 288 of the product's 336 matmuls and DVE is still behind: stops of 1.71 and 1.06 us. In the second layer the last block product waits for DVE's sum that reads its bank (line 1237). In the first, DVE's row of that sum ends at 366.42, so PE, done at 364.21, would have waited there too; what it meets first are the four matmuls of `w_out`, whose operand ACT splits only from 365.25 on. DVE had that operand at 363.49, but ACT's split of a unit ahead of it had waited 1.77 us for PE. e_half, in which DVE has room there, has no such stop, and neither have e_norecip and e_warm, in which 24 matmuls of `w_out` stand at this place.
- *The rivals.* Full clock falls with the rows at 0.50, a shorter wait with the stops of 6.26 and 8.02, weights too late with e_noforms, in which the same units arrive in time, and with ACT's rows in after, none of which waits for a transfer around the product. *The forms come in time* was forecast at 1462.5, and e_noforms, which has this without the work, took 1460.74; e_formsfirst and e_order show that an order that brings the first form in time does not bring that gain, which the prediction had left open.

What was meant to be hidden is not hidden: the forms' 24 us of DVE, 12 in each layer, stand in one queue between the second root and `w_out`, and PE comes to each date of that queue earlier than DVE. An earlier root, or work taken out ahead of the first date, shortens its stop (e_root, e_noadd, e_norecip); work behind it does not (e_half, e_pooladd); another order moves the stop to another date (e_order, e_formsfirst), and so does a first form that PE does not wait for (e_plain). What stays open is whether an order exists in which all dates are met: e_root, e_order, b3 and e_formsfirst are the ones tried, e_order and b3 with a unit that came late.
